# A hybrid decoder block on one core: turned signs in the weights' sums, first and third sums by accumulating DMAs, one-input operations on GpSimd, one plain slab at the FFN's entrance, and L2 in seven products

## The chip, the cores and the metric

The kernel runs on one core of a Trainium2 chip. The time is the device time of one execution, in microseconds; the figure shown is the median of three runs. A profiled execution of the same kernel gives the trace.

## The reference

One decoder block on 512 tokens of width 1024, with 16 meta tokens ahead, all in float32. Cut to what is computed:

```python
u = rmsnorm(h, mix_norm_w)
q, k, v, g_ret, lru_in, lru_gate, gate_a, gate_b = split(u @ w_in)      # eight blocks of 1024 columns
o = chunk_retention(rotary(q), rotary(k) * 128**-0.5, v)                # 8 heads of 128
y_ret = (silu(g_ret) * headnorm(o)) @ w_branch_ret
c = causal_depthwise_conv(lru_in, conv_w, conv_b)                       # width 4
r, i = sigmoid(c @ wa + ba), sigmoid(c @ wx + bx)                       # 4 blocks of 256
a = exp(-8 * r * softplus(-lam))
hs = scan(h = a*h + sqrt(1 - a*a) * (i*c))                              # over the tokens
y_lru = (gelu(lru_gate) * hs) @ w_branch_lru
h = h + (sigmoid(gate_a) * y_ret + sigmoid(gate_b) * y_lru) @ w_out
g, up = split(rmsnorm(h, ffn_norm_w) @ w_ffn_in)                        # hidden 2816
h = h + (silu(g) * up) @ w_ffn_out
return rmsnorm(h, final_norm_w)
```

## The kernel before, in words

**Products.** Every float32 operand is cut into a high part `hi` (a cast to fp32r, on ScalarE, ACT) and a low part `lo` (the difference, on VectorE, DVE). A product is then three products on TensorE (PE), hi*hi, hi*lo and lo*hi: lines 442 to 444 (`mm3`) and 452 to 454 (`block`).

**Weights.** A weight matrix comes in slabs of 128x2048, each of four pieces of 128x512, `a21 a22 a11 a12`. A *plain* slab (`plain`) cuts its four pieces and takes 96 products of 256 columns. A slab in *seven products* (`fast`, `fast512`; Strassen's scheme in Winograd's form) is seen as a 2x2 matrix and takes 84: its seven pieces are `a12 a11 a22` and four sums, `s1 = a21 + a22`, `s3 = a11 - a21`, `s2 = s1 - a11`, `s4 = a12 - s2`, and on the other side stand the activations' blocks `b21 b11 b22` and sums `t1 t3 t2 t4`, which `sums_of` makes once for all slabs of a stage (lines 650 to 667). The results gather in two banks, named `zw...` and `yx...`, and are combined with the small tiles `ws pz u2`.

Each piece goes through `emit` and `weights`: load (SP's queue) into a `raw` buffer, cast (`hi`, L361) and difference (`lo`, L367), with a ring of 9 `hi` and 9 `lo` buffers. A sum is made on DVE by `combine` (L286, buffers of tag `sum`), or by `added`: one load on SP's queue (L297) of the first quarter into a buffer of tag `acc` (4 of them), then an accumulating DMA from GpSimd's queue (POOL, L291) that adds the other quarter. Before, `s1` of the w_in slabs and both first sums of the last two w_fi slabs are made in the second way.

**Order.** PLAN names the steps: R0 to R3 (retention, each a K, Q, G slab), A0 to A3 and B0 to B3 (the two merge gates), I0 to I3 (the recurrent branch's input, followed by `conv`), L0 to L3 (its gelu gate), T0 to T3 (the recurrence's own gates, `lru_gates`), BR and BL (the two branch products). The FFN has 22 slabs of w_fi (`ffn_gate` after each), then w_fo. Slower work (the sums of activations, conv, recurrence) is put on a list by `defer` and let out in pieces by `tick` as products are written. A scheduler then fixes the final order on each engine; no engine runs out of order afterwards.

**FFN entrance.** FIRST = 2 slabs of w_fi are plain. `token_half(0)` multiplies them with the first half of the tokens, `token_half(1)` with the second; the sums t1 to t4 are made meanwhile. From slab 2 on come slabs in seven products.

**Recurrence.** Per block of 256 channels, in two halves of 128x528: d = (1+a)*tanh on DVE (L1261), Sqrt on ACT (`lookup`, L400), a = 1-d on DVE (L1263), then L1269, L1270 and the scan L1272 on DVE. The conv is one `tensor_scalar` (L1207) and three `scalar_tensor_tensor` (L1209) per half.

Of the kernel before, what the change touches and what calls it, by code (L numbers as in the profile page):

```python
# [17 lines left out]
P = 128  # L18
D = 1024
# [23 lines left out]
FIRST = 2  # L43
# [27 lines left out]
PLAN = "R0 R1 R2 R3 A0 A1 A2 A3 I0 BR I1 T0 L0 I2 T1 L1 I3 T2 L2 L3 T3 B0 B1 B2 B3 BL"  # L71

PLAIN_R = "K0 G0".split()
PLAIN_L = "I3 L0 L2 L3".split()
NORM, LAST_NORM = 2.0, 3.7
SUM = 2.0

# [82 lines left out]
def hybrid_block(ctx: ExitStack, tc: tile.TileContext, a: dict):  # L160
# [43 lines left out]
    for step in PLAN.split():  # L204
        if step in ("BR", "BL"):
            order += [(f"w_{step.lower()}", hf) for hf in range(2)]
# [22 lines left out]
    for n, (key, i) in enumerate(order):  # L229
# [71 lines left out]
    def emit(n, later=False):  # L301
# [10 lines left out]
        elif apart and c == "s3":  # L312
            combine(key, i, "s3", a11(), a21(), ALU.subtract)
        elif apart and c in ("s2", "s4"):
            t = kept[key, i]
            if (key, i, "s2") not in sums:
                sums[key, i, "s2"] = t
                nc.vector.tensor_tensor(t, t, a11(), op=ALU.subtract)
            if c == "s4":
                combine(key, i, "s4", a12(), t, ALU.subtract)  # L320
        elif key == "w_fi" and c == "s1":
            for j in (i, i + 1):
                if BY_DMA <= j < NJ and (key, j, "s1") not in sums:
# [7 lines left out]
        elif c == "s1":  # L331
# [6 lines left out]
            combine(key, i, "s3", a11(), a21(), ALU.subtract)  # L338
            s2 = combine(key, i, "s2", s1, a11(), ALU.subtract)
            combine(key, i, "s4", a12(), s2, ALU.subtract)  # L340
# [60 lines left out]


# [54 lines left out]
    def fast(key, s, X, n, banks, name, used):  # L457
# [14 lines left out]
        block(y, part("a12"), X["b21"], n, True)  # L472
        used("b21")
        block(x, part("a11"), X["b11"], n, own)
        used("b11")
# [65 lines left out]
    def branch(key, source, done):  # L541


        parts = {}
        for hf in range(2):
            acc = [bank(f"{key}{hf}_{c}") for c in range(4)]
            for k in range(KT):
                i = k // 2
                if i not in parts:
                    f = source(i)  # L550
                    parts[i] = get(D, F32R), get(D, F32R)
                    split(parts[i], f)
                    put(f)
                w = weights((key, i, k % 2 + 2 * (1 - hf)))[0]
                xh, xl = (p[:, k % 2 * SEQ:(k % 2 + 1) * SEQ] for p in parts[i])
                for c in range(4):
                    mm3(acc[c], *(p[:, c * P:(c + 1) * P] for p in w), xh, xl, k == 0, k == KT - 1)
                if hf == 1 and k % 2 == 1:
                    put(*parts.pop(i))
            for c in range(4):  # L560
                done(4 * hf + c, acc[c])
# [269 lines left out]
    def rotate(x, n, banks=()):  # L831
# [40 lines left out]
    def values(g):  # L872
# [142 lines left out]
    def ret_project(s):  # L1015
        if s == 0:
# [7 lines left out]
            sums = defer(sums_of(UF, U, UV, TH), 0.0)  # L1024
# [7 lines left out]
        if plain_slab("w_in", K + s):  # L1032
            outs = [[bank(f"k{s}_{j}{n}")[:, :TH] for n in range(2)] for j in range(2)]
            plain("w_in", K + s, TH, outs, UV)
            rotate(k4, TH, [(j, slice(n, n + 1), outs[j][n]) for j in range(2) for n in range(2)])
# [164 lines left out]
    def conv(b, xp, x3):  # L1200
# [3 lines left out]
        for j in range(2):  # L1204
            k = 2 * b + j
            cw = [vec[:, V_CW + i * 8 + k:V_CW + i * 8 + k + 1] for i in range(4)]
            nc.vector.tensor_scalar(c3[:, j], x3[:, j], cw[3], vec[:, V_CB + k:V_CB + k + 1], ALU.mult, ALU.add)  # L1207
# [34 lines left out]
    def recurrence(group):  # L1242
# [13 lines left out]
        yield STEPS[0]  # L1256
        for b, r, g, c in group:
            for j in range(2):
                a, t = two(A[b])[:, j], two(r)[:, j]
                d = get(T)  # L1260
                nc.vector.scalar_tensor_tensor(d, a, 1.0, t, ALU.add, ALU.mult)  # L1261
                lookup(t, t, AF.Sqrt)
                nc.vector.tensor_scalar(a, d, -1.0, 1.0, ALU.mult, ALU.add)  # L1263
# [17 lines left out]
    def lru_gate(s):  # L1281
# [379 lines left out]
```

## Time and profile before

| | |
|---|---|
| runs, us | 893.55, 893.53, 893.03; median 893.53 |
| the profiled execution, us | 894.48 |
| its span in the trace, us | 892.7 |
| mean granted PE clock | 0.998 |
| busy, us: DVE, ACT, POOL | 728.3, 511.8, 100.0 |
| where the stages lie, us from the start | I1 to T2 about 300 to 400; L2, L3, T3 about 395 to 420; B gates 420 to 475; FFN's plain slabs 552 to 577; its seven-product slabs from 577 |

The span is one execution from its first instruction to its last; the profiled execution's own time is 1.8 us longer than its span. Instructions are grouped by line, engine and tile. The page's busy shares are means over stages with different limits, so the windows by stage, further down, say more of what a moved instruction meets.

### The profile page before, as it was taken

The numbers are of one execution on the slowest core, as the hardware profiler recorded it, in microseconds if no ns is written. First come the engines' busy times: TensorE is split into PE (matmuls) and PEld (weight loads), VectorE is DVE, ScalarE is ACT, GpSimd is POOL, SyncE is SP. The second block draws the span as 40 slices with busy tenths as digits, with TensorE's granted clock in tenths as the row PEclk, the third lists the DMA queues.
The fourth block names the chain that finished last, engine by engine and source line by source line (L and its number), as shares of the span: only waits on it lengthen the run. The fifth ranks groups of instructions, "written<-read, shape, count | busy, mean of one in ns | idle before, by whom it ended". The sixth has DMA issues, their size and how long they took to land.

```text
span 892.7 us, 17031 instructions
## 1 busy us (share of the span) xinstructions
PE 880.9 (99%) x6398; PEld 832.6 (93%) x6398; DVE 728.3 (82%) x1217; ACT 511.8 (57%) x964; POOL 100.0 (11%) x147
## 2 busy tenths in 40 slices
PE   8999999999999999999999999999999999999996
PEld 7999999999998899999998888999999999988885
DVE  5997898899778479897985427999999998999973
ACT  6655655657564248869763315555556555665653
POOL 3312310122200000000000220000000000111112
PEclk9999999999999999999999999999999999999999
DMA  9734244454354333432482322133333334685622
GB/s 316 209 127 117 74 119 130 116 145 131 84 138 146 95 130 85 129 108 74 134 259 93 97 78 93 50 106 112 115 96 106 109 113 141 181 226 155 131 48 94
DMA packets 59587, 111.75 MB, mean 125 GB/s; under 512 B 6752, under 2 KB 7008, under 8 KB 59504
## 3 DMA queue, kind: packets, MB, share of 16 engines
q1 hardware_dynamic: 51872, 95.68, 33.4%
q0 software_dynamic: 6048, 11.01, 7.4%
q10 hardware_dynamic: 1584, 3.97, 1.4%
q8 instruction: 50, 0.82, 0.4%
q14 instruction: 33, 0.27, 0.1%
HBM read 108.54 MB, written 2.10 MB: 124 GB/s over the span
## 4 chain that ended last, share of the span: by engine, by line
PE 96%; DVE 1%; issue 1%; ACT 1%; DMA 1%; POOL 0%; POOLq 0%; ACTq 0%; DVEq 0%
PE zwf L453 4%; PE zwf L454 4%; PE zwf L452 4%; PE fo L443 4%; PE fo L444 4%; PE fo L442 4%; PE yxf L452 3%; PE yxf L454 3%; PE yxf L453 3%; PE w_bl L442 2%; PE wo L444 2%; PE wo L443 2%; PE w_bl L443 2%; PE w_br L442 2%; PE w_br L444 2%; PE w_bl L444 2%
## 5 line engine op out<-in xcount | busy, mean ns | idle before, releaser
L454 PE MATMUL zwf<-b,lo 128*128 128x256 f32 x320 | 90.1, 282 | 0.0
L453 PE MATMUL zwf<-b,hi 128*128 128x256 f32 x320 | 89.9, 281 | 0.0
L452 PE MATMUL zwf<-b,hi 128*128 128x256 f32 x320 | 89.6, 281 | 0.0
L361 ACT CAST hi<-s_w_in 128x512 fp32r<-128x512 f32 x88 | 54.4, 621 | 58.0 <-PE w_br L443 6.5
L361 ACT CAST hi<-raw_w_in 128x512 fp32r<-128x512 f32 x90 | 55.5, 620 | 43.1 <-PE w_br L443 8.5
L361 ACT CAST hi<-s_w_fi 128x512 fp32r<-128x512 f32 x80 | 49.7, 621 | 50.2 <-PE zwf L453 35.2
L367 DVE TENSOR_TENSOR lo<-s_w_in,hi 128x512 fp32r<-128x512 f32 x88 | 59.8, 686 | 17.4 <-ACT hi L361 16.3
L367 DVE TENSOR_TENSOR lo<-raw_w_in,hi 128x512 fp32r<-128x512 f32 x90 | 60.8, 684 | 10.8 <-ACT hi L361 10.6
L452 PE MATMUL yxf<-b,hi 128*128 128x256 f32 x240 | 67.5, 281 | 0.0
L453 PE MATMUL yxf<-b,hi 128*128 128x256 f32 x240 | 67.4, 281 | 0.0
L454 PE MATMUL yxf<-b,lo 128*128 128x256 f32 x240 | 66.6, 281 | 0.0
L367 DVE TENSOR_TENSOR lo<-s_w_fi,hi 128x512 fp32r<-128x512 f32 x80 | 54.9, 687 | 13.2 <-ACT hi L361 13.0
L361 ACT CAST hi<-raw_w_fi 128x512 fp32r<-128x512 f32 x68 | 41.9, 622 | 34.8 <-PE yxf L453 20.3
L452 PEld LDWEIGHTS zwf<-b,hi 128*128 128x128 f32 x320 | 60.5, 189 | 0.0
L454 PEld LDWEIGHTS zwf<-b,lo 128*128 128x128 f32 x320 | 60.4, 189 | 0.0
L453 PEld LDWEIGHTS zwf<-b,hi 128*128 128x128 f32 x320 | 60.4, 189 | 0.0
L443 PE MATMUL fo<-lo,b 128*128 128x512 f32 x158 | 59.1, 393 | 0.0
L442 PE MATMUL fo<-hi,b 128*128 128x512 f32 x158 | 57.5, 393 | 0.0
L444 PE MATMUL fo<-hi,b 128*128 128x512 f32 x158 | 56.0, 393 | 0.0
L367 DVE TENSOR_TENSOR lo<-raw_w_fi,hi 128x512 fp32r<-128x512 f32 x68 | 46.4, 685 | 4.1 <-ACT hi L361 3.4
L509 DVE TENSOR_TENSOR b<-b,b 128x512 fp32r<-128x512 f32 (+3 forms) x58 | 46.4, 809 | 1.0 <-ACT b L508 0.9
L452 PEld LDWEIGHTS yxf<-b,hi 128*128 128x128 f32 x240 | 45.3, 189 | 0.0
(447 smaller groups left out, 3147.4 us busy)
## 6 DMA issues: line engine op xcount, KB each, us to landing
raw_w_in<-in_w_in SPq DMA_DIRECT2D x112, 256.0 KB, 3.2
raw_w_fi<-in_w_fi SPq DMA_DIRECT2D x86, 256.0 KB, 3.1
raw_w_fo<-in_w_fo SPq DMA_DIRECT2D x44, 256.0 KB, 4.2
s_w_in<-in_w_in SPq DMA_DIRECT2D x20, 256.0 KB, 3.0
s_w_in<-in_w_in POOLq DMA_DIRECT2D x20, 256.0 KB, 5.4
raw_w_br<-in_w_br SPq DMA_DIRECT2D x16, 256.0 KB, 3.3
raw_w_bl<-in_w_bl SPq DMA_DIRECT2D x16, 256.0 KB, 4.5
raw_w_out<-in_w_out SPq DMA_DIRECT2D x16, 256.0 KB, 2.9
```

The source lines that it names most:

```text
L361: highs.append(nc.scalar.copy(hi, src))
L367: return engine.tensor_tensor(lo, src, hi.bitcast(F32), op=ALU.subtract)
L442: nc.tensor.matmul(out, wh, xh, start=start, stop=False, skip_group_check=True)
L443: nc.tensor.matmul(out, wh, xl, start=False, stop=False, skip_group_check=True)
L444: nc.tensor.matmul(out, wl, xh, start=False, stop=stop, skip_group_check=True)
L452: nc.tensor.matmul(out, wh, xh, start=start and i == 0, stop=False, skip_group_check=True)
L453: nc.tensor.matmul(out, wh, xl, start=False, stop=False, skip_group_check=True)
L454: nc.tensor.matmul(out, wl, xh, start=False, stop=i == 3, skip_group_check=True)
L509: low = engine.tensor_tensor(lo, src, hi.bitcast(F32), op=ALU.subtract)
```

## The change

Five things:

1. **Signs.** All weight sums become additions: `s3 = a11 + a21`, `s2 = s1 + a11`, `s4 = a12 + s2`, with the activations' sums taken for negated blocks (`sums_of(..., True)`). Half of each result then comes out negated, and the sign is put right where it is read: in the lookups (`lookup_turned`: two of 512 columns for one of 1024), in the conv's coefficients (`less`), in the rotation, in the values.
2. **Sums by DMA.** With additions only, `s3` of the w_in slabs too is made by `added`, so a slab has two accumulating DMAs where it had one, in the same four buffers. `s1` and `s3` of w_fi 1 to 3 are made so as well (SOON = 3).
3. **GpSimd** takes the conv's first `tensor_scalar` and the recurrence's `a = 1-d`; Sqrt now goes first, into a tile of its own.
4. **FFN entrance.** One plain slab (FIRST = 1). Of the next two, the products `a12*b21` and `a11*b11` are moved ahead, between the two token halves (`first_products`, AHEAD_OF = 2).
5. **L2** is no longer among the plain slabs of L. BL's two halves become steps of their own, in the same place.

```diff
-FIRST = 2
+FIRST = 1
+AHEAD_OF = 2
+SOON = 3
...
-PLAIN_L = "I3 L0 L2 L3".split()
+PLAIN_L = "I3 L0 L3".split()
+SUMS_BY_DMA = (("s1", 1), ("s3", 2))
...
+        elif key == "w_fi" and i < FIRST + AHEAD_OF:
+            if i == FIRST:
+                pieces += [(key, j, c) for j in range(FIRST, FIRST + AHEAD_OF) for c in FAST[2:4]]
+            pieces += [(key, i, c) for c in FAST if c not in FAST[2:4]]
...
             for m in [m for m in order[k + 1:k + 5] if m[0] == "w_in" and not plain_slab(*m)][:1]:
-                sums[(*m, "s1")] = added(*m, "s1", 0, 1)
+                for name, other in SUMS_BY_DMA:
+                    sums[(*m, name)] = added(*m, name, 0, other)
...
-            s1 = sums[key, i, "s1"]
-            combine(key, i, "s3", a11(), a21(), ALU.subtract)
-            s2 = combine(key, i, "s2", s1, a11(), ALU.subtract)
-            combine(key, i, "s4", a12(), s2, ALU.subtract)
+            if (key, i, "s3") not in sums:
+                combine(key, i, "s3", a11(), a21(), ALU.add)
+            s2 = combine(key, i, "s2", sums[key, i, "s1"], a11(), ALU.add)
+            combine(key, i, "s4", a12(), s2, ALU.add)
...
+    def lookup_turned(x, f, scale=1.0):
+        for j in range(2):
+            part = x[:, j * SEQ:(j + 1) * SEQ]
+            lookup(part, part, f, scale=-scale if j else scale)
...
+    def first_products(key, s, X, name):
+
+        yx = bank(f"yx{name}{s}")
+        for half, (c, b) in enumerate((("a12", "b21"), ("a11", "b11"))):
+            block(yx[:, half * 256:(half + 1) * 256], weights((key, s, c))[0], X[b], 256, half == 0)
+        return yx
...
-            nc.vector.tensor_scalar(c3[:, j], x3[:, j], cw[3], vec[:, V_CB + k:V_CB + k + 1], ALU.mult, ALU.add)
+            nc.gpsimd.tensor_scalar(c3[:, j], x3[:, j], cw[3], vec[:, V_CB + k:V_CB + k + 1], ALU.mult, ALU.add)
...
-                d = get(T)
-                nc.vector.scalar_tensor_tensor(d, a, 1.0, t, ALU.add, ALU.mult)
-                lookup(t, t, AF.Sqrt)
-                nc.vector.tensor_scalar(a, d, -1.0, 1.0, ALU.mult, ALU.add)
-                put(d)
+                d = roots[b, j] = get(T)
+                lookup(d, t, AF.Sqrt)
+                nc.vector.scalar_tensor_tensor(t, a, 1.0, t, ALU.add, ALU.mult)
+                nc.gpsimd.tensor_scalar(a, t, -1.0, 1.0, ALU.mult, ALU.add)
...
-                nc.vector.scalar_tensor_tensor(t, a, 1.0, t, ALU.add, ALU.mult)
-                nc.vector.tensor_tensor(g1, g1, t, op=ALU.mult)
+                nc.vector.scalar_tensor_tensor(d, a, 1.0, d, ALU.add, ALU.mult)
+                nc.vector.tensor_tensor(g1, g1, d, op=ALU.mult)
...
     token_half(0)
+    yxs = {j: first_products("w_fi", j, VV, "f") for j in range(FIRST, FIRST + AHEAD_OF)}
     drain()
     item = defer(sums_of(VF, VX, VV, 256, True), 0.0)
     token_half(1)
...
-        fast512("w_fi", j, VV, gu, "f", last_use if j == NJ - 1 else lambda b: None)
+        fast512("w_fi", j, VV, gu, "f", last_use if j == NJ - 1 else lambda b: None, yxs.get(j))
```

How the order moves at three places follows; numbers in a tile's name only number it, and lines are those of the kernel that is shown.

*DVE at the FFN's entrance*, before: `b` are the activations' sums and their low parts (L665), `s_w_fi` and `lo` the weights'.

```order
L665 TENSOR_TENSOR b_7032<-b_6491,b_7031 128x1024
L657 TENSOR_TENSOR b_6493<-b_6494,b_6493 128x1024
L637 TENSOR_TENSOR b_6502<-b_6494,b_6501 128x4x128
L661 SCALAR_TENSOR_TENSOR b_6494<-b_6491,b_6494 128x1024
L665 TENSOR_TENSOR b_7059<-b_6493,b_7058 128x1024
L661 SCALAR_TENSOR_TENSOR b_6492<-b_6494,b_6492 128x1024
L367 TENSOR_TENSOR lo_7045<-s_w_fi_6899,hi_7044 128x512
L665 TENSOR_TENSOR b_7090<-b_6494,b_7089 128x1024
L367 TENSOR_TENSOR lo_7066<-raw_w_fi_3_6903,hi_7065 128x512
```

And after, where the low parts of t1 to t4 are made by L688:

```order
L378 TENSOR_TENSOR lo_6986<-s_w_fi_6855,hi_6985 128x512
L378 TENSOR_TENSOR lo_6990<-s_w_fi_6912,hi_6989 128x512
L684 SCALAR_TENSOR_TENSOR b_6501<-b_6498,b_6501 128x1024
L688 TENSOR_TENSOR b_7102<-b_6500,b_7101 128x1024
L378 TENSOR_TENSOR lo_6996<-raw_w_fi_1_6993,hi_6995 128x512
L295 TENSOR_TENSOR s_w_fi_7023<-raw_w_fi_3_6882,s_w_fi_7021 128x512
L378 TENSOR_TENSOR lo_7000<-s_w_fi_6910,hi_6999 128x512
L684 SCALAR_TENSOR_TENSOR b_6499<-b_6501,b_6499 128x1024
L378 TENSOR_TENSOR lo_7026<-s_w_fi_6876,hi_7025 128x512
L688 TENSOR_TENSOR b_7125<-b_6501,b_7124 128x1024
```

Between the activations' sums now stand twice as many of the weights' splits and sums (of slabs 1 and 2).

*GpSimd in the last two blocks of the recurrence and the B gates*, before: only the accumulating DMAs for s1.

```order
L291 DMA s_w_in_4290<-in_w_in 128x512
L291 DMA s_w_in_5281<-in_w_in 128x512
L291 DMA s_w_in_5556<-in_w_in 128x512
L291 DMA s_w_in_5695<-in_w_in 128x512
L291 DMA s_w_fi_9435<-in_w_fi 128x512
```

And after: two of them per slab, with the conv's (L1239) and the recurrence's (L1296) operations between.

```order
L300 DMA s_w_in_5318<-in_w_in 128x512
L300 DMA s_w_in_5321<-in_w_in 128x512
L1239 TENSOR_SCALAR b_5120<-b_4982,vec 128x528 x2
L1296 TENSOR_SCALAR b_5217<-b_5114 128x528
L300 DMA s_w_in_5566<-in_w_in 128x512
L1296 TENSOR_SCALAR b_5217<-b_5114 128x528
L300 DMA s_w_in_5569<-in_w_in 128x512
L300 DMA s_w_in_5703<-in_w_in 128x512
L300 DMA s_w_in_5706<-in_w_in 128x512
L1296 TENSOR_SCALAR b_5592<-b_5494 128x528 x2
```

The recurrence's operations now stand in POOL's queue behind DMAs that wait for their base loads.

*PE between the two token halves*, before: after the last transposes (`hT`) come the products of the second plain slab (`f` with hi_6847).

```order
L453 MATMUL f_1_6912<-b_6498,hi_6822 128x256
L454 MATMUL f_1_6912<-b_6497,lo_6823 128x256
L647 MATMUL hT_0_6951<-b_6889,b_6486 128x128 x4
L647 MATMUL hT_1_6959<-b_6889,b_6486 128x128 x4
L452 MATMUL f_0_6913<-b_6495,hi_6847 128x256
```

And after, where the first token half ends and the products moved ahead begin (`yxf`, slab 1):

```order
L468 MATMUL f_1_6919<-b_6504,hi_6829 128x256
L469 MATMUL f_1_6919<-b_6505,hi_6829 128x256
L470 MATMUL f_1_6919<-b_6504,lo_6830 128x256
L468 MATMUL yxf_6984<-b_6504,hi_6860 128x256
L469 MATMUL yxf_6984<-b_6505,hi_6860 128x256
```

The second plain slab's place is taken by products of the slabs 1 and 2 that need no sum of activations; the transposes now stand ten products earlier, inside the first slab.

More of the change, by code (lines that the diff above doesn't have):

```diff
@@ L204, in hybrid_block @@
     for step in PLAN.split():
-        if step in ("BR", "BL"):
-            order += [(f"w_{step.lower()}", hf) for hf in range(2)]
+        if step == "BR":
+            order += [("w_br", hf) for hf in range(2)]
+        elif step[:2] == "BL":
+            order.append(("w_bl", int(step[2])))
         elif step[0] == "R":
@@ L471, in fast @@
         used("t3")
[L472 to L475, printed above, removed]
+        if not begun:
+            block(y, part("a12"), X["b21"], n, True)
+            used("b21")
+            block(x, part("a11"), X["b11"], n, own)
+            used("b11")
         nc.scalar.copy(ws[:, :n], w_)
@@ L539, in plain512, with branch @@
         return pbs
[L541 to L559, printed above, removed]
-            for c in range(4):
-                done(4 * hf + c, acc[c])
+    halves_of = {}
+    def branch(key, hf, source, done):
+        acc = [bank(f"{key}{hf}_{c}") for c in range(4)]
+        for k in range(KT):
+            i = k // 2
+            if i not in halves_of:
+                f = source(i)
+                halves_of[i] = get(D, F32R), get(D, F32R)
+                split(halves_of[i], f)
+                put(f)
+            w = weights((key, i, k % 2 + 2 * (1 - hf)))[0]
+            xh, xl = (p[:, k % 2 * SEQ:(k % 2 + 1) * SEQ] for p in halves_of[i])
+            for c in range(4):
+                mm3(acc[c], *(p[:, c * P:(c + 1) * P] for p in w), xh, xl, k == 0, k == KT - 1)
+            if hf == 1 and k % 2 == 1:
+                put(*halves_of.pop(i))
+        for c in range(4):
+            done(4 * hf + c, acc[c])
     def whole_branch(key, source, done):
@@ L829, in hybrid_block, with rotate @@
     R = [None] * 4
-    def rotate(x, n, banks=()):
+    def rotate(x, n, banks=(), sign=1.0):
         tmp = get(4 * n)
@@ L1034, in ret_project @@
             plain("w_in", K + s, TH, outs, UV)
-            rotate(k4, TH, [(j, slice(n, n + 1), outs[j][n]) for j in range(2) for n in range(2)])
+            rotate(k4, TH, [(j, slice(n, n + 1), outs[j][n]) for j in range(2) for n in range(2)],
+                   -1.0 if not plain_slab("w_in", Q + s) else 1.0)
         else:
@@ L1205, in conv @@
             k = 2 * b + j
-            cw = [vec[:, V_CW + i * 8 + k:V_CW + i * 8 + k + 1] for i in range(4)]
-            nc.vector.tensor_scalar(c3[:, j], x3[:, j], cw[3], vec[:, V_CB + k:V_CB + k + 1], ALU.mult, ALU.add)
+            turned = j == 1 and not plain_slab("w_in", LI + b)
+            cw = [less[:, i * 8 + k:i * 8 + k + 1] if turned else vec[:, V_CW + i * 8 + k:V_CW + i * 8 + k + 1] for i in range(4)]
+            nc.gpsimd.tensor_scalar(c3[:, j], x3[:, j], cw[3], vec[:, V_CB + k:V_CB + k + 1], ALU.mult, ALU.add)
             for i in range(1, 4):
@@ L1325, in hybrid_block @@
             whole_branch("w_br", lambda i: R[i], gated(macc, GA))
-        elif step == "BL":
-            for b in list(U):
-                put(*U.pop(b))
-            branch("w_bl", recurred, merged)
+        elif step[:2] == "BL":
+            s = int(step[2])
+            if U and not [p for p in plan[plan.index(step):] if p[:2] != "BL"]:
+                for b in list(U):
+                    put(*U.pop(b))
+            branch("w_bl", s, recurred, merged)
         elif step[0] == "A":
```

53 lines of the change are left out of this document (31 added, 22 removed).

## The prediction, as it stood before the run

> **What bounds the kernel now.** I read four views in this order: the page's busy shares, TensorE's (PE's) waits, the windows by stage, and the chain that ended last. First the page, its parts 1 and 4:
>
> ```profile
> PE 880.9 (99%) x6398; PEld 832.6 (93%) x6398; DVE 728.3 (82%) x1217; ACT 511.8 (57%) x964; POOL 100.0 (11%) x147
> PE 96%; DVE 1%; issue 1%; ACT 1%; DMA 1%; POOL 0%; POOLq 0%; ACTq 0%; DVEq 0%
> ```
>
> PE is busy for 880.9 of 892.7 us and carries 96% of the chain. Its waits, all of them:
>
> ```profile
> PE warm L192 <- POOL ident masks.py:199: 2.9, 1, 2.9
> PE v L443 <- DVE lo L367: 0.6, 2, 0.4
> PE v L442 <- ACT b L710: 0.3, 1, 0.3
> PE v L444 <- DVE b L715: 0.2, 1, 0.2
> ```
>
> These are 4.0 us, and all lie at the program's start (the warm-up and the values' first slab), which the change hardly touches. So there is no waiting to win back: the time falls only if PE gets fewer products, and it rises with every hole that the change opens. How near the holes are, the windows tell (per engine busy us and count):
>
> ```profile
> 340.00:400.00 60.00, 60.00 (x502) 60.00 (x502) 56.98 (x97) 45.74 (x81) 0.86 (x1) 1.00 0.35 111
> 400.00:440.00 40.00, 39.92 (x336) 39.72 (x335) 33.52 (x51) 35.22 (x59) 1.73 (x2) 1.00 0.27 80
> 440.00:460.00 20.00, 20.00 (x151) 19.15 (x150) 19.91 (x30) 14.79 (x26) 0.86 (x1) 1.00 0.81 236
> 560.00:580.00 20.00, 20.00 (x170) 20.00 (x170) 19.40 (x26) 12.65 (x19) 0.00 (x0) 1.00 0.17 54
> 560.00:740.00 180.00, 180.00 (x1522) 180.00 (x1522) 165.47 (x266) 103.73 (x195) 0.00 (x0) 1.00 0.32 101
> ```
>
> The columns are length, PE, PEld, VectorE (DVE), ScalarE (ACT), GpSimd (POOL), clock, DMA share, GB/s. PE is full everywhere at a clock of 1.00; DVE is close behind: 95% in the Griffin branch's slabs (340 to 400), 100% in the second half of the B gates (440 to 460), 97% at the FFN's entrance (560 to 580), 92% in its slabs (560 to 740). In the first three the diff moves work. One place is close to open, by the chain between 425 and 445:
>
> ```profile
> 428.58 0.14 DVE lo L367
> ...
> 434.59 0.69 DVE s_w_in L286
> ...
> 435.88 1.18 DVE b L1272
> ...
> 438.03 0.62 ACT hi L361
> ...
> 438.97 0.39 PE yxgate L452
> ```
>
> For 10 us the chain leaves PE and goes through splits, a sum of weights, a scan of the recurrence (L1272) and a cast; yet PE misses only 0.08 us (39.92 of 40.00 busy): what DVE makes there is ready just when it is wanted.
>
> **The change part by part.** *Products removed.* L2 and the FFN's slab 1 go from the plain form (96 products of 256 columns) to the seven-product form (84): 24 fewer. The window 560:740 is of such products alone, 1522 in 180.00 us, 118 ns each; 24 x 118 ns = 2.8 us. This is the whole direct gain, 0.3%, and it is on the path wherever PE stays fed.
>
> *What L2 costs elsewhere.* Seven pieces for four are three more casts and three more splits, two more sums (s2, s4), and three evictions. All this stands on ACT and DVE:
>
> ```profile
> L361 ACT CAST hi<-raw_w_in 128x512 fp32r<-128x512 f32 x90 | 55.5, 620 | 43.1 <-PE w_br L443 8.5 <-PE yxq L453 4.6 <-PE yxgate L453 3.2
> L367 DVE TENSOR_TENSOR lo<-raw_w_in,hi 128x512 fp32r<-128x512 f32 x90 | 60.8, 684 | 10.8 <-ACT hi L361 10.6
> L286 DVE TENSOR_TENSOR s_w_in<-raw_w_in,raw_w_in 128x512 f32<-128x512 f32 x24 | 16.3, 683 | 1.4 <-DMA raw_w_in<-in_w_in 1.2
> L1207 DVE TENSOR_SCALAR b<-b,vec 128x528 f32<-128x528 f32 x8 | 4.2, 546 | 0.0
> L1263 DVE TENSOR_SCALAR b<-b 128x528 f32<-128x528 f32 x8 | 3.4, 429 | 0.1
> ```
>
> DVE: five of 0.68 and evictions of about 1.7, 5.1 us. ACT: 1.9 us, in windows where it has an eighth to a quarter free. Against it DVE gives away the conv's first operation (8 x 0.55) and the recurrence's (8 x 0.43), 7.8 us over the four blocks, and the third sum of nearly each seven-product slab of w_in (in the x24 row, 0.68 each). Around the chain's gap (the four B gates) that is 4 x 0.68 + 4 x 0.43 = 4.4 us less DVE work in about 45 us, which hides what L2 adds just ahead of it. So on DVE alone the narrow place becomes wider, and I cost L2 at nothing.
>
> *Work that goes to GpSimd.* No row of before has a one-input operation of 128x528 there. The nearest are:
>
> ```profile
> L729 POOL TENSOR_SCALAR b<-ident,rx 128x128 f32<-128x128 f32 x4 | 3.0, 748 | 0.4
> L367 POOL TENSOR_TENSOR lo<-raw_w_out,hi 128x512 fp32r<-128x512 f32 x8 | 11.4, 1431 | 64.3 <-ACT hi L361 60.0 <-PE w_bl L443 4.3
> L291 POOL DMA_DIRECT2D s_w_in<-in_w_in x20 | 17.9, 904 | 183.2 <-DMA s_w_in<-in_w_in 64.5 <-DVE b L1189 30.2 <-DVE lo L367 21.3
> s_w_in<-in_w_in SPq DMA_DIRECT2D x20, 256.0 KB, 3.0
> s_w_in<-in_w_in POOLq DMA_DIRECT2D x20, 256.0 KB, 5.4
> ```
>
> So 0.75 us (same operation, a quarter of the width) to 1.43 (same width, two inputs); I take 1.1, between the two, since it has the width of one and the single input of the other. In the recurrence the operation sits on a chain of Sqrt (ACT), product (DVE), 1-d (POOL), product (DVE), scan: it was 0.43 on DVE and is now 1.1 and two handovers, some 0.9 us later per half. Behind that chain wait only the scans and the merge, and the order puts two or three weight splits between, so DVE doesn't stand still for it unless POOL is late.
>
> *Sums by accumulating DMA.* Each such sum is a load on SP's queue (3.0 us), then the accumulating one, 0.9 us of POOL's issue and 5.4 until it lands: 9 to 10 us. With both sums of a slab in four buffers the lead is two slabs instead of four. For the last B slab the load waits for the split of slab 29, and the s2 that needs it stands 16 DVE operations later, 10 to 12 us by 0.6 to 0.7 each: 1 to 2 us to spare. POOL's one-input operations of the last block stand behind the second issue: they start 3.0 + 2 x 0.9 = 4.8 us after the split and end at 5.9, where DVE, after seven operations, wants the first result at 4.2: 1.7 us late. Against the 4.4 us won there I cost it at nothing to 1 us.
>
> *Signs.* They change operands, not counts; two half lookups of 128x512 for one of 128x1024 cost ACT 0.2 us each, on an engine with room:
>
> ```profile
> L400 ACT ACTIVATE b<-b 128x1024 f32<-128x1024 f32 x12 | 12.7, 1060 | 2.3 <-DVE b L495 2.1
> L400 ACT ACTIVATE b<-b 128x512 f32<-128x512 f32 x20 | 12.7, 633 | 1.2 <-DVE b L495 1.2
> ```
>
> *The FFN's entrance.* The second plain slab was the cover under which DVE made the activations' sums t1 to t4 and the first weights of seven products. DVE's timeline before (start, length):
>
> ```profile
> 562.03 1.23 DVE L665 TENSOR_TENSOR b<-b,b 128x1024 fp32r<-128x1024 f32 x1
> ...
> 566.16 1.22 DVE L665 TENSOR_TENSOR b<-b,b 128x1024 fp32r<-128x1024 f32 x1
> 567.30 1.22 DVE L661 SCALAR_TENSOR_TENSOR b<-b,b 128x1024 f32<-128x1024 f32 x1
> ...
> 572.71 1.22 DVE L665 TENSOR_TENSOR b<-b,b 128x1024 fp32r<-128x1024 f32 x1 [0.24 <-ACT b L664]
> 573.85 0.68 DVE L367 TENSOR_TENSOR lo<-raw_w_fi,hi 128x512 fp32r<-128x512 f32 x1
> 574.45 0.68 DVE L367 TENSOR_TENSOR lo<-s_w_fi,hi 128x512 fp32r<-128x512 f32 x1
> ...
> 552.04 0.36 PE L452 MATMUL f<-b,hi 128*128 128x256 f32 x1
> 557.80 0.94 PE L647 MATMUL hT<-b,b 128*128 128x128 f32 x7
> 576.68 0.28 PE L452 MATMUL zwf<-b,hi 128*128 128x256 f32 x1
> ```
>
> The plain products begin at 552.04, the last transposes run at 557.80, and the first seven-product block at 576.68, 13 us after t1 was split (562.03 + 1.23). From start to start a DVE operation takes 0.60 us at 512 columns and 1.14 at 1024. After the change the transposes come after 38 products, at 552.04 + 38 x 0.118 = 556.5; 10 plain products, 48 of the products moved ahead and 48 plain ones fill PE to about 569.9, then 24 of slab 1, so the first s2 (with t2) at 572.7 and slab 2's s2 at 577. In DVE's new order the split of t2 is the 17th operation behind the transposes (7 wide, 10 narrow: 14.0 us), that of slab 2's s2 the 24th (8 wide, 16 narrow: 18.7). From 557.1 to 557.6, with half a microsecond of idle as before, they end at 571.4 to 572.1 and 576.0 to 576.9. Both are in time, by about 1 us each. I take 0.5 us lost (0 to 2).
>
> **The sum.** -2.8 (24 products) + 0 to 1 (gates) + 0 to 2 (entrance), likeliest +0.5 in all: -2.3. The profiled execution took 894.48 and becomes 892.2; the median of the runs is 893.53, 0.95 lower, and becomes 891.2. From no change such a measurement can be told at 0.2%, 1.8 us, so up to 891.7 is faster.
>
> **The rivals.** *B, the entrance gives it back.* DVE is busy without a break there (19.40 of 20), and 1 us is all that covers it; if the casts of t1 to t4 or GpSimd's rr row come 2 us later than I set them, PE stands 1 to 3 us: -2.8 + 1 to 3, 891.7 to 893.7. For it: the cover falls by 24 products and by the early splits. Against: the products moved ahead need nothing of t1 to t4.
>
> *C, GpSimd and DVE in each other's way: slower.* Before has two places where a GpSimd operation runs beside a wide one of DVE:
>
> ```profile
> 485.31 1.48 POOL L367 TENSOR_TENSOR lo<-raw_w_out,hi 128x512 fp32r<-128x512 f32 x1 [35.16 <-ACT hi L361]
> 484.43 1.22 DVE L1306 TENSOR_TENSOR b<-b,b 128x1024 f32<-128x1024 f32 x1
> 485.56 3.45 DVE L509 TENSOR_TENSOR b<-b,b 128x1024 fp32r<-128x1024 f32 x2
> ```
>
> Two wide operations that take 1.14 + 1.22 alone took 3.45: 1.1 us longer, about as long as GpSimd was still at work. If each of the 16 moved operations holds DVE so for its 1.1 us, the move costs DVE 17.6 us and saves 7.8. The B gates have four of GpSimd's: 4.4 us of holding eat the 4.4 us won, and the waits behind the accumulating DMAs (1.7 us, twice) come on top where the chain has 0.1 us to spare. With the conv's two beside them (2.2): holes of 2 to 6 us, -2.8 + 2 to 6, 892.7 to 896.7, middle 894.9. It decides the sign from 2.8 us of holes on. The Trainium skill says so too: by "SBUF — State Buffer", section "Who interferes with whom", a DVE instruction with two SBUF inputs and a GpSimd one that reads SBUF exclude each other, and the one issued second is blocked for the whole of the first; by that rule the sum would be this rival's, and the two places above agree with it (1.1 us). Against C: between 400 and 440 DVE has 16% of its time free, where a hold costs nothing.
>
> *D, late sums.* If an accumulating DMA takes 12 us instead of 9 (the buffers are in use longer than I count), s2 of three or four gate slabs is late by 1 us each: -2.8 + 3 to 4, 893.7 to 894.7. The early slabs had 35 us of lead and could lose most of it.
>
> **How the numbers follow.** A, PE fed but for 0 to 1 us, 890.7 to 891.7: 0.55. B: 0.24. C: 0.15. D: 0.06. The likeliest gives 891.2; the range runs from 890.3 (no loss, and two tenths in the handovers) to 894.9, C's middle. Faster by over 0.2%: A and the near edge of B, 0.56; within 0.2%: most of B, C's lower third and half of D, 0.30; slower: the rest of C and D, 0.14.
>
> **What would show it.** PE's busy count falls by 24 products and its busy time by 2.8 us; its waits stay near 4.0 us. A row "PE yxf <- DVE lo" or "zwf <- DVE lo" near 570 to 585 shows B. DVE rows of two inputs that are longer than 0.70 (narrow) or 1.25 (wide) beside GpSimd's shows C, with waits of PE on the gates' weights between 420 and 450. Waits of DVE's sums on a DMA of s_w_in show D. I am wrong if PE's count falls and the span does not, with no wait in any of these places.

## The result: 898.27 us, half a percent slower

| | median, us | runs | ratio to before |
|---|---|---|---|
| before | 893.54 | 893.03 to 893.82 | 1 |
| after | 898.27 | 898.0 to 899.39 | 1.0054 [1.0043, 1.0066] |

The forecast was 891.2 us, with the range 890.3 to 894.9: 7.1 us too low. Parts 1 and 4 of the page after, in the order in which those of before were shown:

```profile
PE 879.7 (98%) x6374; PEld 829.6 (92%) x6374; DVE 717.8 (80%) x1191; ACT 516.7 (58%) x989; POOL 143.2 (16%) x193
PE 85%; DVE 5%; DMA 3%; ACT 3%; issue 2%; POOL 2%; POOLq 0%; ACTq 0%; DVEq 0%
```

PE has its 24 products fewer (6398 to 6374), DVE 10.5 us less work, and yet the chain leaves PE for 15% of the span instead of 4%. PE's waits after:

```profile
PE zwlg L468 <- DVE pzlg L494: 1.4, 2, 1.1
...
PE yxq L468 <- ACT pzq L495: 0.9, 1, 0.9
PE zwgate L468 <- DVE pzgate L494: 0.9, 1, 0.9
PE zwg L468 <- DVE b L1165: 0.7, 1, 0.7
PE yxgate L468 <- ACT pzgate L495: 0.5, 1, 0.5
PE zli L468 <- DVE pzli L494: 0.5, 1, 0.5
PE yxgate L470 <- DVE lo L378: 0.4, 1, 0.4
PE zwlg L468 <- DVE b L1228: 0.3, 1, 0.3
...
PE zwlg L468 <- DVE b L1220: 0.2, 1, 0.2
```

Nearly all are for banks of PSUM, the memory into which PE writes, that nobody had emptied: `zwlg`, `yxq`, `zwgate`, `yxgate` and `zli` wait for the evictions `pz...`, by which ACT or DVE empties a bank. The prediction had looked for weights. The windows of the prediction, after:

```profile
340.00:400.00 60.00, 58.70 (x482) 57.88 (x481) 53.56 (x86) 46.20 (x83) 15.63 (x12) 1.00 0.42 112
400.00:440.00 40.00, 37.52 (x311) 36.92 (x310) 32.37 (x48) 34.17 (x59) 7.19 (x8) 1.00 0.49 124
440.00:460.00 20.00, 19.53 (x160) 18.95 (x159) 20.00 (x30) 14.10 (x26) 3.51 (x4) 1.00 0.69 190
560.00:580.00 20.00, 20.00 (x173) 20.00 (x172) 18.03 (x24) 13.09 (x20) 2.81 (x4) 1.00 0.43 110
560.00:740.00 180.00, 180.00 (x1527) 180.00 (x1526) 166.24 (x269) 104.12 (x197) 6.30 (x8) 1.00 0.39 118
```

DVE is relieved where the prediction said (56.98 to 53.56 us in 340 to 400), and there PE idles. The FFN's entrance is full. By the starts of the first product of each stage in PE's timeline, us:

| | to the first zwq | R stage, to w_br | I, L, T, B, to w_bl | to wo | wo, FFN in, to fo | rest |
|---|---|---|---|---|---|---|
| before | 53.5 | 217.6 | 184.2 | 48.9 | 267.2 | 121.4 |
| after | 52.8 | 219.6 | 189.4 | 48.9 | 265.3 | 121.6 |

The entrance's stage became 1.9 us shorter. The R stage became 2.1 us longer, for which the prediction's sum had nothing. The stage of the Griffin branch and the B gates became 5.2 us longer, though it has 12 products (1.4 us) less to do. That is 6.6 us of holes (time in which PE stands) more than before, where the sum had 0 to 1. (The last gate products of before start between 463.4 and 464.8 us, so its B gates run from 420 to 465 and not to 475, and the last of them stand behind w_bl's first.)

### The profile page after: what moved, and what is told of

Read it like the earlier page. It is cut to its first block, busy times and chain, and to the rows that moved or that the text cites. A ratio compares the mean times of both kernels' runs of the same rounds, so it can differ in the third digit from the quotient of the medians.

```text
span 897.6 us, 17098 instructions
## 1 busy us (share of the span) xinstructions
PE 879.7 (98%) x6374; PEld 829.6 (92%) x6374; DVE 717.8 (80%) x1191; ACT 516.7 (58%) x989; POOL 143.2 (16%) x193
## 4 chain that ended last, share of the span: by engine, by line
PE 85%; DVE 5%; DMA 3%; ACT 3%; issue 2%; POOL 2%; POOLq 0%; ACTq 0%; DVEq 0%
PE zwf L469 4%; PE zwf L470 4%; PE zwf L468 4%; PE fo L460 4%; PE fo L459 4%; PE fo L458 4%; PE yxf L469 3%; PE yxf L468 3%; PE yxf L470 3%; DMA raw_w_in<-in_w_in 2%; PE w_bl L458 2%; PE wo L460 2%; PE w_bl L459 2%; PE wo L459 2%; PE w_br L460 2%
## 5 line engine op out<-in xcount | busy, mean ns | idle before, releaser
L469 PE MATMUL zwf<-b,hi 128*128 128x256 f32 x336 | 94.4, 281 | 0.0
L470 PE MATMUL zwf<-b,lo 128*128 128x256 f32 x336 | 94.3, 281 | 0.0
L468 PE MATMUL zwf<-b,hi 128*128 128x256 f32 x336 | 93.9, 280 | 0.0
L378 DVE TENSOR_TENSOR lo<-s_w_in,hi 128x512 fp32r<-128x512 f32 x92 | 63.2, 691 | 16.9 <-ACT hi L372 16.4
L469 PE MATMUL yxf<-b,hi 128*128 128x256 f32 x252 | 70.7, 281 | 0.0
L468 PE MATMUL yxf<-b,hi 128*128 128x256 f32 x252 | 70.6, 281 | 0.0
L470 PE MATMUL yxf<-b,lo 128*128 128x256 f32 x252 | 70.3, 281 | 0.0
L300 POOL DMA_DIRECT2D s_w_in<-in_w_in x44 | 38.9, 900 | 187.2 <-DMA s_w_in<-in_w_in 85.7
L378 DVE TENSOR_TENSOR lo<-s_w_fi,hi 128x512 fp32r<-128x512 f32 x84 | 57.5, 686 | 12.3 <-ACT hi L372 10.4
L468 PEld LDWEIGHTS zwf<-b,hi 128*128 128x128 f32 x336 | 63.4, 189 | 0.0
L469 PEld LDWEIGHTS zwf<-b,hi 128*128 128x128 f32 x336 | 63.3, 188 | 0.0
L470 PEld LDWEIGHTS zwf<-b,lo 128*128 128x128 f32 x336 | 63.3, 189 | 0.0
L532 ACT CAST b<-b 128x512 fp32r<-128x512 f32 (+3 forms) x58 | 39.3, 690 | 15.5 <-DVE b L1241 9.4
```

Source lines behind the costliest of these rows:

```text
L300: state["added"] = behind(nc.gpsimd.dma_start(t, a[key][i][:, c * Q4:(c + 1) * Q4], accum_op=ALU.add), state.get("added"))
L378: return engine.tensor_tensor(lo, src, hi.bitcast(F32), op=ALU.subtract)
L468: nc.tensor.matmul(out, wh, xh, start=start and i == 0, stop=False, skip_group_check=True)
L469: nc.tensor.matmul(out, wh, xl, start=False, stop=False, skip_group_check=True)
L470: nc.tensor.matmul(out, wl, xh, start=False, stop=i == 3, skip_group_check=True)
L532: high = nc.scalar.copy(hi, src)
```

## The experiments

All times are medians. "Holes" below are the time from w_br to w_bl above 183.9 us (L2 plain, in f6, where PE stands nowhere in that stage) or above 182.5 us (L2 in seven products, 1.4 us less work). They come from the one profiled execution of each kernel, which can lie off its median: that of e2 took 896.22 us (median 897.91), that of after 899.39 (898.27). The kernel before ran beside each, at 893.5 to 893.7.

**One part undone at a time.**

```diff
 # e1: s3 on DVE again
-SUMS_BY_DMA = (("s1", 1), ("s3", 2))
+SUMS_BY_DMA = (("s1", 1),)
 # e2: one-input operations on DVE again
-            nc.gpsimd.tensor_scalar(c3[:, j], ...
+            nc.vector.tensor_scalar(c3[:, j], ...
-                nc.gpsimd.tensor_scalar(a, t, -1.0, ...
+                nc.vector.tensor_scalar(a, t, -1.0, ...
 # e3: L2 plain again
-PLAIN_L = "I3 L0 L3".split()
+PLAIN_L = "I3 L0 L2 L3".split()
 # e4: e1 and e2 together
```

> The changed kernel, but s3 of the w_in slabs is again summed on DVE (one accumulating DMA per slab instead of two; w_fi 1 to 3 keep theirs); signs, GpSimd's operations, the FFN's entrance and L2 stay changed. Theory Q (queue): the second sum's base load waits on SP's queue for one of four buffers, and the plain loads of weights behind it come late; then the 7.7 us of holes shrink to 1 or 2 and the time is 891.5 to 893. Theory G (GpSimd): the conv's and the recurrence's operations there delay the chain of the recurrence; then holes stay, 897 to 898.5. Theory L (L2's extra pieces overfill DVE and ACT between 380 and 440): DVE has even more to do, 898 to 900.

> The changed kernel, but the conv's first operation and the recurrence's 1-d are back on DVE; both sums by DMA stay. Theory Q: the SP queue is as before, the holes stay or grow a little by 7.8 us of DVE work, 897.5 to 899.5. Theory G: the holes between 340 and 460 (6.5 us) shrink to 1 or 2, 892.5 to 894. Theory L: 898 to 900.

> The changed kernel with L2 plain again, 12 products more (+1.4 us) and four weight pieces instead of seven. Theory L: the holes between 380 and 445 (about 4 us) go, 895 to 896. Theories Q and G: they stay but for a little, 897.5 to 899.5.

> Both back on DVE: s3 of the w_in slabs, and the conv's and the recurrence's one-input operations; what stays is the signs, the FFN's entrance and L2 in seven products. Theory Q: DVE then has 5 us more than before between 340 and 460 where it was 92% busy, 892 to 895, slower than with s3 alone taken back. Theory G: 891 to 893, the fastest of these. Theory L: 896 to 899.

Measured: e1 896.37, e2 897.91, e3 893.83, e4 891.26 (0.9973 [0.9962, 0.9984]). None of the theories stands alone: the first two undone singly bring 1.9 and 0.4 us, together 7.0, and L2 alone brings 4.4 although it adds 1.4 us of products. e4, without the moves off DVE, comes to the time that was forecast for the whole change. That is a coincidence: the forecast counts 1.4 us for L2, which f6 below finds to be worth nothing here. Of these four, e4 gives DVE the most work. The windows 340 to 460 of e3 and e4, in this order:

```profile
340.00:460.00 120.00, 119.71 (x982) 118.29 (x981) 107.47 (x163) 96.20 (x167) 25.01 (x20) 1.00 0.45 124
```

```profile
340.00:460.00 120.00, 119.62 (x972) 117.89 (x972) 112.20 (x183) 98.10 (x172) 5.17 (x6) 1.00 0.44 128
```

DVE is 94% busy in e4 and PE has 0.4 us of idle time. So DVE's busy share alone doesn't open the holes.

**Which of GpSimd's operations.** Both have s3 on DVE as e1; f1 has the conv's operation back too (the first line pair of e2), f2 the recurrence's (the second).

> The changed kernel with s3 and the conv's first operation back on DVE; the recurrence's 1-d stays on GpSimd. With s3 alone taken back it was 896.4 us, with s3 and both operations 891.3: 5.1 us lie in the two. If the recurrence's chain (Sqrt, product, 1-d, product, scan, each on another engine) carries them, 895 to 896.5; if the conv's operation does (before its three DVE operations and the cast for which ACT stands), 891 to 892.5; if the two share them, 893 to 894.5.

> The mirror: s3 and the recurrence's 1-d back on DVE, the conv's first operation stays on GpSimd. Recurrence guilty: 891 to 892.5; conv guilty: 895 to 896.5; shared: 893 to 894.5.

Measured: f1 896.87, f2 893.05. Beside e4, the recurrence's 1-d costs 5.6 us on GpSimd, the conv's operation 1.8. In the traces the order hardly differs: 1164 of f1's 1221 DVE instructions stand in the order of e4.

**What the sums by DMA change (e2 against e4, 6.6 us).** In the trace after, DVE stands 3.32 us before the s2 sum of L2. First DVE's timeline (start, length, operation, idle time before it in brackets), then that of SP's queue:

```profile
359.49 0.67 DVE L378 TENSOR_TENSOR lo<-s_w_in,hi 128x512 fp32r<-128x512 f32 x1
363.47 0.69 DVE L295 TENSOR_TENSOR s_w_in<-s_w_in,raw_w_in 128x512 f32<-128x512 f32 x1 [3.32 <-DMA raw_w_in<-in_w_in]
```

```profile
353.00 0.33 SPq L290 DMA_DIRECT2D raw_gates<-in_gates  x1
355.90 2.06 SPq L306 DMA_DIRECT2D s_w_in<-in_w_in  x2
358.58 0.33 SPq L290 DMA_DIRECT2D raw_gates<-in_gates  x1
359.18 18.13 SPq L290 DMA_DIRECT2D raw_w_in<-in_w_in  x7
```

The accumulated sum is there. The plain piece a11, which s2 adds, went out at 359.18, behind two base loads and a gate. Behind DVE's sum stand the evictions of the li banks. Three ways to help the loads, all from e2:

```diff
 # f3: bases on GpSimd's queue
-        nc.sync.dma_start(t, ...          (in added)
+        nc.gpsimd.dma_start(t, ...
 # f4: six buffers for these sums      RING, RAW, SUMS, ACC, LOOK
-... = 9, 8, 3, 4, 8
+... = 9, 8, 2, 6, 8
 # g1: ten raw buffers
-... = 9, 8, 3, 4, 8
+... = 9, 10, 2, 4, 8
```

> Both one-input operations on DVE, both sums by DMA (the run of that kind gave 897.9), and here the base loads of the sums go out from GpSimd's queue instead of SP's, so no load of a plain piece stands behind one that waits for a buffer. Theory Q (SP's queue is blocked): DVE's waits for plain pieces between 340 and 460 fall below 1 us, time 892 to 894.5. Rival (two sums in four buffers are late by themselves, whoever issues the base): 896.5 to 898.5.

> As the run with both operations on DVE and both sums by DMA (897.9), but with six buffers for these sums instead of four and two instead of three for DVE's sums: three slabs of lead instead of two. If the buffers are what the base loads wait for, with theory Q or with its rival: 891.5 to 894. If neither: 896.5 to 899, and the two buffers for DVE's sums may cost a little.

> Both one-input operations on DVE, both sums by DMA (897.9 as it stands), with ten raw buffers for plain pieces instead of eight and two for DVE's sums instead of three. In that run, with six sum buffers, and with the bases on another queue alike, DVE stood 2.0 to 3.1 us near 363 for the a11 piece of L1 and PE 1.1 us behind it, though the sums were in time. Theory R (the raw buffers hold the loads back, and the s2 sum then blocks DVE's queue ahead of the evictions PE waits for): the wait near 363 goes, 892 to 894.5. Rival (the fixed order on ACT and DVE carries the rest, the load is only one sign of it): 896 to 898.

Measured: f3 903.62, f4 897.53, g1 894.29. f3 loses 5.5 us before the R stage (3.1 of them in one wait of PE for GpSimd's L752) and keeps the wait for a11 (2.83 us): SP's queue as such is not it. More sum buffers do nothing. With more raw buffers the wait is gone (none over 0.6 us is left between 340 and 460) and 3.6 us of time with it. Holes fall from 4.6 to 2.7.

Whose sum is it? Counted over the trace (each slab in seven products has one s2, one s4 and four splits of its sums), it is L2's, made 17 us ahead of L2's first split, and so is the next, s4 at 368.14, for which DVE waits 0.96 us. (The expectation of g1 calls the piece L1's.) With L2 plain, in before and in e3, DVE makes no sum of weights between 348 and 384, and in e3, with both sums by DMA, it waits only 0.2 us for plain pieces between 340 and 460. With L2 in seven products the place in DVE's order decides what the wait costs. In e1 and e4 L2's sum stands behind the evictions of the li banks: DVE waits 1.93 and 0.60 us for a plain piece, and PE has no hole there. In after, e2, f3 and f4 it stands ahead of them, and PE waits 0.2 to 1.0 us for the evictions. That the sums by DMA put it there is not shown; g6, below, has it with s3 on DVE.

**The recurrence's form and its tiles.**

```diff
 # g3 (from f1, 1-d on GpSimd) and g4 (from e4, 1-d on DVE): the order of before
-                d = roots[b, j] = get(T)
-                lookup(d, t, AF.Sqrt)
-                nc.vector.scalar_tensor_tensor(t, a, 1.0, t, ALU.add, ALU.mult)
-                nc.gpsimd.tensor_scalar(a, t, -1.0, 1.0, ALU.mult, ALU.add)
+                d = get(T)
+                nc.vector.scalar_tensor_tensor(d, a, 1.0, t, ALU.add, ALU.mult)
+                lookup(t, t, AF.Sqrt)
+                nc.gpsimd.tensor_scalar(a, d, -1.0, 1.0, ALU.mult, ALU.add)     # g4: nc.vector
+                put(d)
 # g5 (from f1): 33 large buffers
-SLOTS = 32
+SLOTS = 33                             # and SUMS 3 -> 2
```

> s3 and the conv back on DVE, 1-d on GpSimd (896.9 so), but in the order of before: product first, Sqrt in place, and the tile d given back after 1-d instead of after the second product. Theory B (buffers: the lookups of the last gates wait for a tile that the recurrence gives back late, and the B gates wait for their banks): 891.5 to 894. Theory H (handovers: GpSimd's 1.2 us and its two semaphores per half lengthen the chain, whatever the tiles): 895.5 to 898.

> As the 896.9 run (s3 and conv on DVE, 1-d on GpSimd, Sqrt first), with 33 instead of 32 of the large buffers and two instead of three for DVE's sums. Theory B: the lookups of the last gates find a free tile, the holes near 419 go, 892 to 895. Theory H: 896 to 898.

> The best version so far (s3, conv and 1-d on DVE: 891.3) with the recurrence in the order of before. If Sqrt in a tile of its own shortens the chain: 892 to 894 here. If its longer-held tile costs more than it wins (theory B): 890 to 891.2. If neither: 891.0 to 891.6.

Measured: g3 893.11, g5 896.35, g4 893.75. One more large buffer wins 0.5 us, so theory B (a tile given back late) is not supported. In the order of before, 1-d needs only the product, so it can run beside Sqrt, and on GpSimd it costs no more than on DVE (893.11 against 893.75). In the changed order the product overwrites the tile that Sqrt reads, so 1-d comes after Sqrt, and there it costs 5.6. Sqrt first is worth 2.5 us with 1-d on DVE and loses 3.8 with it on GpSimd.

**All moves with both cures, and the size of the two gains.**

```diff
 # h1 (from after): RAW, SUMS = 10, 2 as g1, and the recurrence as g3
 # f6 (from e4)
-PLAIN_L = "I3 L0 L3".split()
+PLAIN_L = "I3 L0 L2 L3".split()
 # f5 (from e4)
-FIRST, AHEAD_OF, SOON: 1, 2, 3
+FIRST, AHEAD_OF, SOON: 2, 0, 0
```

> The change as it was made (898.3), all of its moves kept, with two cures: ten raw buffers and two for DVE's sums, and the recurrence in the order of before, so that GpSimd's 1-d runs beside ACT's Sqrt instead of after it. Singly the first took 3.6 us from the run with both operations on DVE, the second 3.8 us from the run with s3 and the conv on DVE. If these two are the causes and add up: 890 to 892. If the conv's move or the sums have a price of their own in the fixed order: 892.5 to 895. If the cures don't carry over: 896 to 898.

> The best version (s3, conv and 1-d on DVE, 891.3) with L2 plain again: 12 products more, 1.4 us, less the 0.9 us of holes that it has between 340 and 460. If L2 in seven products is worth its products there: 892.2 to 893. If its holes eat the gain: 890.8 to 891.8.

> The best version with two plain slabs at the FFN's entrance again: 12 products more. By the prediction's step (the entrance loses 0 to 2 us of its 1.4): 891 to 892.7. By the trace after, where PE has no hole between 540 and 600: 892.6 to 893.

Measured: h1 895.3, f6 891.31, f5 892.83. The two cures together bring 3.0 us, not 7. The entrance is worth 1.57 us in e4, its 12 products (1.4) and a little more. L2 in seven products is worth nothing even in the best version: 891.26 with it, 891.31 without. Four of the runs make a table:

| | L2 in seven products | L2 plain |
|---|---|---|
| s3 by DMA, both operations on GpSimd | 898.27 (after) | 893.83 (e3) |
| s3 and both operations on DVE | 891.26 (e4) | 891.31 (f6) |

The moves off DVE cost 7.0 us with L2 in seven products and 2.5 with L2 plain. L2 in seven products costs 4.4 us with the moves and nothing without them. So 4.5 us of the loss come only where the two meet.

**How much is the order alone.** In g6 and h3 no operation is added, removed or moved to another engine.

```diff
 # g6 (from e4)            RING, RAW, SUMS, ACC, LOOK
-... = 9, 8, 3, 4, 8
+... = 9, 9, 3, 4, 8
 # h3 (from e4)
-... = 9, 8, 3, 4, 8
+... = 9, 8, 2, 4, 8
 # h4 (from f1)
-PLAIN_L = "I3 L0 L3".split()
+PLAIN_L = "I3 L0 L2 L3".split()
```

> The best version with nine raw buffers instead of eight. If raw buffers still hold loads back there (0.6 to 1.2 us of DVE's waits for plain pieces): 890.3 to 891. If not: 891 to 891.6.

> The best version (891.3) with two instead of three buffers for DVE's sums: no operation is added, removed or moved to another engine, but the fixed order changes (773 of DVE's 1219 rows). One raw buffer more, also no operation, had cost it 4.5 us. If the order is a lottery of several us in itself: anything from 892.5 to 896. If that one was an exception and the order is good for a range of buffers: 890.8 to 892.2.

> 1-d on GpSimd after Sqrt as in the 896.9 run (s3 and conv on DVE), with L2 plain. Theory I (the two meet: the recurrence's longer chain only reaches PE because L2 in seven products takes 1.4 us of PE's cover and adds five DVE operations and three evictions just ahead of it): 891.5 to 893. Theory H alone (the chain is late by itself): 895.5 to 898.

Measured: g6 895.81, h3 894.84, h4 892.65. With L2 in seven products a buffer more or less moves the time by 3.6 to 4.5 us, against both expectations for g6. In g6 one place alone costs 1.8 us: s3 and s2 of L2 now stand ahead of the li banks' evictions on DVE and wait for a plain piece, and PE waits for the evictions (DVE's row, then PE's):

```profile
362.38 0.69 DVE L295 TENSOR_TENSOR s_w_in<-raw_w_in,raw_w_in 128x512 f32<-128x512 f32 x1 [2.20 <-DMA raw_w_in<-in_w_in]
365.33 0.39 PE L468 MATMUL zwlg<-b,hi 128*128 128x256 f32 x1 [1.78 <-DVE b L1220]
```

With L2 plain, 1-d on GpSimd after Sqrt costs 1.3 us (h4 against f6) instead of 5.6 (f1 against e4).

By the holes in the stage from w_br to w_bl, the runs with L2 plain lie at the low end:

| | holes, us |
|---|---|
| L2 plain: f6, before, h4, e3 | 0, 0.3, 1.2, 1.3 |
| L2 in seven products: e4 and f5, g3, h1, g1, f2, g4, h3, f3, e2, g6, f4, e1, f1, after | 1.2 both, 2.5, 2.6, 2.7, 2.9, 3.2, 4.0, 4.4, 4.6, 5.0, 5.2, 6.5, 6.7, 6.9 |

(g5 is left out: 24 of the stage's products lie outside its border there.) With L2 in seven products, all but e4 and f5 lose more than the 1.4 us that L2's products are worth.

Where do the holes lie? A slab in seven products has a wait of its own that a plain one has not: the product with s4 goes on in the bank of the product with s1, and before it DVE must have read that bank into `pz`. In after this makes the stage's largest hole. ACT's copy of the other half was there by 400.3 and the bank was full since 397; on DVE the eviction stands behind a conv operation that waits for GpSimd, the rest of the conv and three splits (DVE's two rows, then PE's):

```profile
398.18 0.77 DVE L1241 SCALAR_TENSOR_TENSOR b<-b,vec,b 128x527 f32<-128x527 f32 x1 [0.61 <-POOL b L1239]
...
403.81 0.42 DVE L494 TENSOR_TENSOR pzlg<-zwlg,wslg 128x256 f32<-128x256 f32 x1
...
404.28 0.39 PE L468 MATMUL zwlg<-b,hi 128*128 128x256 f32 x1 [1.10 <-DVE pzlg L494]
```

Waits for such `pz`, of which DVE makes one half and ACT the other (slabs I2, L1, L2 and the B gates), are 3.3 of the 4.2 us of PE's waits that the list above has for this stage. (The rest of its 6.9 us are gaps too short for the list, and a slower start after each wait: the product that comes then takes 0.39 us, others 0.28.)

The other place is the handover from T3 to the B gates, whose first bank waits for ACT's first lookup on the last `gt`. For f6, e4 and f1 in turn, ACT's row of the timeline and then PE's:

```profile
415.34 0.48 ACT L411 ACTIVATE b<-gt,vec 128x264 f32<-128x264 f32 x1
418.66 0.28 PE L468 MATMUL zwgate<-b,hi 128*128 128x256 f32 x1
```

```profile
416.79 0.48 ACT L411 ACTIVATE b<-gt,vec 128x264 f32<-128x264 f32 x1 [0.39 <-DVE b L1302]
417.32 0.39 PE L468 MATMUL zwgate<-b,hi 128*128 128x256 f32 x1 [0.35 <-ACT b L411]
```

```profile
420.63 1.22 ACT L411 ACTIVATE b<-gt,vec 128x264 f32<-128x264 f32 x3
421.17 0.39 PE L468 MATMUL zwgate<-b,hi 128*128 128x256 f32 x1 [1.30 <-ACT b L411]
```

With L2 plain, in f6, the lookup starts 3.3 us ahead of the product (before: 415.98 and 419.28, the same 3.3). This is the lead. With seven products PE would come at 416.97 (417.32 less its wait), 1.7 us sooner, and the lookup starts 1.45 later: 0.2 us ahead, and PE waits. The lookups are later because on ACT they stand behind L2's gelu, which no longer reads PSUM but what DVE has gathered from it, and behind the recurrence of block 2 (DVE L1302). In f1 the same lookup is 3.8 us later still. PE waits for it in twelve of the sixteen profiles with L2 in seven products (0.3 to 2.3 us) and in none with L2 plain. In after it is late too; ACT's timeline has ahead of it

```profile
397.06 0.63 ACT L532 CAST b<-b 128x528 fp32r<-128x528 f32 x1 [3.40 <-DVE b L1241]
...
403.38 0.63 ACT L532 CAST b<-b 128x528 fp32r<-128x528 f32 x1 [2.59 <-DVE b L1241]
...
417.70 1.15 ACT L411 ACTIVATE b<-b 128x512 f32<-128x512 f32 x2 [2.31 <-DVE b L519]
...
422.18 1.23 ACT L411 ACTIVATE b<-gt,vec 128x264 f32<-128x264 f32 x3
```

waits for two conv results and for L2's evictions, each late on DVE, with weight casts behind them on ACT. But PE has no hole there: it has stood so long by then, at the banks above, that its product comes at 423.03, 0.85 us behind the lookup.

## Why the prediction was wrong, step by step

**Products removed: right in size.** 24 x 118 ns = 2.8 us. (The window from which the 118 ns are read holds plain products until 576.7, at the same rate.) The entrance's half of it was had in full.

**The FFN's entrance: right.** It was given a loss of 0.5 us (0 to 2); it had none (180.00 of 180.00 from 560 to 740, 1.57 us gained in e4 against f5). Rival B did not come. The margin was thinner than its "about 1 us each": 577 less 576.0 to 576.9 is 0.1 to 1.0 us.

**What L2 costs elsewhere: the step that failed.** "On DVE alone the narrow place becomes wider, and I cost L2 at nothing." DVE did get the relief that this counts on, but it was the wrong account: it adds up DVE's time and doesn't follow the banks that PE needs next. L2 in seven products puts an eviction into the middle of the slab for which PE itself waits (1.10 us in after). It puts sums on DVE ahead of I2's evictions, for whose pieces DVE stands 3.32 and 0.96 us. And it puts two evictions on DVE ahead of a lookup on ACT. It also takes 1.4 us of PE's work away ahead of the handover to the B gates, and a lead of 3.3 us shrank to 0.2 in e4. Its net price was 4.4 us in the change as made (e3), 4.2 with 1-d on GpSimd (f1 against h4), 0 at best (e4 against f6), where the sum had -1.4. The gates' term, 0 to 1 us, became 6.6 us of holes more in that stage.

**Work that goes to GpSimd: duration right, place wrong.** I took 1.1 us for one operation:

```profile
L1296 POOL TENSOR_SCALAR b<-b 128x528 f32<-128x528 f32 x8 | 9.4, 1179 | 34.5 <-DVE b L1295 27.9 <-PE lg L470 6.5
L1239 POOL TENSOR_SCALAR b<-b,vec 128x528 f32<-128x528 f32 x5 | 8.3, 1658 | 27.9 <-DVE b L1220 21.7 <-DVE b L1228 6.2
```

But "behind that chain wait only the scans and the merge" was false: behind it wait the lookups of the next block, in ACT's queue, and behind these the banks of the B gates. The price was 5.6 us for the recurrence and 1.8 for the conv with L2 in seven products, 1.3 for the recurrence with L2 plain.

**Sums by accumulating DMA: 0 to 1 us was too little, and for another reason.** (16 operations of 0.6 to 0.7 us are 9.6 to 11.2, not 10 to 12, so the time to spare was 0.3 to 1.9 us.) Rival D did not come: the sums landed in time (5.1 us after the issue). Late were plain pieces, which DVE awaits for 5.4 us between 340 and 460 (before: none listed), 4.3 of them for the sums of L2. In the R stage, to which the sum gave nothing, PE waited 0.9 us for a bank of `yxq` in all seven profiles with both sums by DMA and in no other. A second hole of that stage, in after alone, is a queue's order (start, length in the chain):

```profile
92.43 0.90 POOL s_w_in L300
...
93.72 1.06 POOL rr_o L1163
...
95.62 0.61 DVE b L1165
96.28 0.39 PE zwg L468
```

The heads' `rr_o` stood on GpSimd behind an accumulating DMA's issue, and PE's next bank behind it.

**Rival C: the sign came as it said, mostly not by its mechanism.** The hold between GpSimd and DVE is there (GpSimd's row, then DVE's):

```profile
412.14 0.91 POOL L1296 TENSOR_SCALAR b<-b 128x528 f32<-128x528 f32 x1 [13.99 <-DVE b L1295]
412.47 1.13 DVE L1295 SCALAR_TENSOR_TENSOR b<-b,b 128x528 f32<-128x528 f32 x1
```

DVE's operation takes 1.13 us instead of 0.70. Beside the sixteen moved operations of after, eight of DVE's rows are longer so, by 0.42 to 0.52 us; with smaller delays that makes 3.8 us. Rival C had 17.6, and the move takes 7.8 off DVE. The Trainium skill's rule ("SBUF — State Buffer", section "Who interferes with whom") agrees with these two rows in kind: DVE's operation, issued second, ends 0.55 us after GpSimd's. By the rule it would end at 413.05 + 0.70 = 413.75 and it ended at 413.60, so the rule holds nearly in size as well. It costs little here since the two overlap only in part.

**What stays open.** With L2 in seven products, a change of buffers alone moves 3.6 to 4.5 us. So the single prices above (1.8, 2.5, 3.6, 3.8, 5.6) hold each for one pair of fixed orders, and may be due to the order and not to the move; how much of them a scheduler could save was not tried. No buffer was changed with L2 plain, so it is not shown that those kernels keep their time through such a change; that they do rests on four profiles. What the traces do show are the waits that they name and the entrance's gain.

## What to carry to other kernels

A busy share says nothing on what a moved operation costs: follow the one buffer or bank that PE needs next, count how far ahead of PE it is emptied (here 3.3 us), and charge every edit to that lead, also the edits that make PE faster. Before a step is moved to an idle engine, see whether it then stands in series with another engine's step or beside it; 3.8 us went with it here, in one pair of orders. When no lead is left, a buffer more or less can move the time more than the edit that is under test, so try such changes, which move no operation, beside it. And take the version with the lead: L2 plain, s3 and the one-input operations on DVE, one plain slab at the entrance gives 891.31 us, the same as the best version found (891.26), with no hole between 340 and 460.

## What the runs showed of the hardware

The recurrence's operation of 128x528 with one input takes 1.18 us on GpSimd (mean of 8) against 0.43 on DVE; a DVE operation with two inputs that is issued beside it takes about 1.13 instead of 0.70. An accumulating DMA of 256 KB lands 5.1 us after its issue on GpSimd's queue (w_in, median of 44). With thirty more DMAs on that queue (42 before, 72 after), w_in's plain loads took 3.4 us in the median instead of 3.2, and w_bl's 7.3 instead of 4.5; why w_bl's did is not known.
